# A two-layer decoder trunk on one core: gate and up with seven-product blocks over 14 of 16 k-tiles, w_down laid between them, one weight sum in four made by an adding transfer

## The chip, the core and the metric

The kernel runs on one core of one Trainium2 chip. The metric is the device time in microseconds (us), the median of several executions. In the profile the engines are PE (TensorE, the matrix products), PEld (its weight loads, which overlap it), DVE (VectorE), ACT (ScalarE), POOL (GpSimd) and SP (SyncE, which here only starts transfers). SBUF is the memory on the chip that the engines read; PSUM holds the eight banks into which PE adds up its products; DRAM holds the inputs.

## What is computed

The reference is a decoder of two layers over 256 tokens of width 2048, in fp32. Each layer has a mixer (layer 0: a Mamba-2 and a latent-attention group side by side; layer 1: stick-breaking attention) and a feed-forward part. Only the feed-forward part is changed in what PE does:

```
def swiglu_ffn(h, w_gate, w_up, w_down):
    return (jax.nn.silu(h @ w_gate) * (h @ w_up)) @ w_down

for layer in range(DEPTH):                    # DEPTH = 2
    h = rms_norm(x, mix_norm[layer])
    mix = ssd_mla_mixer(...) if layer % 2 == 0 else stick_breaking_mixer(...)
    x = x + mix
    x = x + swiglu_ffn(rms_norm(x, ffn_norm[layer]), w_gate[layer], w_up[layer], w_down[layer])
return rms_norm(x, final_norm)
```

`w_gate` and `w_up` are 2048 x 5632 in each layer, `w_down` is 5632 x 2048.

## The kernel before

**Tiles and products.** The 256 tokens are two row tiles of 128 (t = 0, 1). A width of 2048 is 16 k-tiles of 128. The hidden width of 5632 is 11 column groups of 512, n = 0 to 10. A weight piece is four k-tiles of 512 columns: 1 MB, a tile of 128 x 2048. All data is fp32, and PE multiplies words that are rounded to a shorter form (fp32r), so each piece is split: ACT casts it to its high part `wh` (L317), and DVE subtracts that from the piece, which leaves the low part in the piece's own buffer (L323). One product of a k-tile and 512 columns is three matmuls: high by `wh`, low by `wh`, high by the low part. What the text calls a product is one such matmul.

**Gate and up (`pair`).** For each column group the kernel makes four results of 128 x 512: gate and up, each for both row tiles. It looks on this as a 2 x 2 block product (two row tiles by two halves of the k-tiles, two halves by gate and up) and uses the seven products of Strassen's scheme in Winograd's form, M1 to M7, in place of eight. For this it needs four sums of weight pieces (L676, on DVE), which are split like pieces, and sums of the operands, made while the norm before is made. With b11, b21 for the two k halves of gate and b12, b22 for those of up, M1 takes b11, M3 b22 and M2 b21; M5 takes t1 = b12 - b11, M6 t2 = b22 - t1, M4 b21 - t2, and M7 b22 - b12, which is written over b12. The four accumulating banks are called z, p3, p2 and p4, a product's result goes to the bank of the results that need it, and what two results share is copied away from the bank in between by ACT (L750).

**How many k-tiles.** With the order HALF (n = 0, 1, 2) M1 to M7 cover 8 of the 16 k-tiles, and four pieces c0 to c3 with plain products the other eight. With MORE (n = 3 to 10) a second set of seven over 4 more k-tiles (n0 to n4, its half-piece sums t1 to t4) is added, and only c2 and c3 stay plain. With LATE `pair` serves the first columns of the two output projections. Seven blocks over 8 k-tiles are 7 x 4 k-tile products for the four results, where plain products would be 8 x 4.

**w_down.** The hidden activations h (L866 to L872: sum, silu, norm factor, product with up) are copied by a POOL transfer into a buffer of fp32r words (L875), transposed by PE (L328), split and kept as operands. `down` multiplies a pair of column groups (8 k-tiles) by one of the four column blocks of w_down: two pieces, 48 products (L423, L425, L426), then two copies out of PSUM on ACT (L890) and two adding transfers of 256 KB from SBUF into the DRAM buffers `saved` (L891). After each pair n from 2 to 9 two held projections follow. Behind the last pair, four projections of 12 k-tiles (72 products each) end the layer; the residual, which `residual_away` put into `saved`, comes back for them (`residual_back`).

**What sets the order.** PE runs the products in the order in which the code makes them. DVE, ACT, POOL and SP are ordered by a scheduler that follows priorities (`wprio` counts up with each weight piece, copies and h are urgent) and by the buffers: 4 for `wh`, 6 (7 in the feed-forward part) for pieces, 2 (3 in the feed-forward part, with a "lent" one) for sums. A piece's buffer comes free with the last product of its low part, and the next load or sum that gets that buffer waits for it.

## Time and profile before

| | |
|---|---|
| median of 3 runs | 2386.84 us (2384.85 to 2387.33) |
| profiled execution, span from first to last instruction | 2382.8 us |
| granted clock of PE, mean | 0.999 |
| PE busy | 2359.7 us, 99% |
| DVE busy | 1995.9 us, 84% |
| ACT busy | 1460.3 us, 61% |
| POOL busy | 234.9 us, 10% |
| moved by transfers | 497.87 MB, 209 GB/s over the span |

How to read it: a share of busy time is one over the whole span, with the mixers in it. A row of the groups of instructions names line, engine, operation, output<-input with shapes, count, then busy time and mean duration in ns, then the engine's idle time just before them and what ended it. A row of a timeline gives start, duration, engine and line, with the wait in front in brackets.

### The profile page before, as it was taken

How to read it: one execution, taken by the hardware profiler on the slowest of the kernel's cores; microseconds unless marked ns; L12 is line 12 of the kernel's file. 1: busy time of each engine (PE TensorE's matmuls, PEld its weight loads, DVE VectorE, ACT ScalarE, POOL GpSimd, SP SyncE). 2: the span in 40 equal slices, each digit the busy share in tenths (PEclk: the TensorE clock that was granted, in tenths of full speed). 3: DMA queues.
4: the chain of work that ended last, by engine and by line, in shares of the span. 5: the costliest groups of instructions: out<-in, count | busy, mean ns of one | idle time of the engine just before them, and what ended most of it. 6: DMA issues, size and time to landing. Idle time of an engine off the chain costs nothing.

```text
span 2382.8 us, 28019 instructions
## 1 busy us (share of the span) xinstructions
PE 2359.7 (99%) x10948; PEld 1956.2 (82%) x10948; DVE 1995.9 (84%) x1654; ACT 1460.3 (61%) x1476; POOL 234.9 (10%) x301
## 2 busy tenths in 40 slices
PE   8999999999999999999999999999999999999998
PEld 7888888887888888888888888888888888888886
DVE  6776587588997989989887889779998888999884
ACT  6665565565765655666665686775665565656663
POOL 1342011110000000000010010000000000000011
PEclk9999999999999999999999999999999999999999
DMA  7655556445667777777776555556667777777773
GB/s 265 198 187 195 181 194 191 127 142 177 230 212 231 222 225 232 231 226 231 225 251 204 203 177 176 177 177 230 230 225 209 237 230 225 226 228 234 226 257 114
DMA packets 274901, 497.87 MB, mean 209 GB/s; under 512 B 22924, under 2 KB 48144, under 8 KB 274768
## 3 DMA queue, kind: packets, MB, share of 16 engines
q1 hardware_dynamic: 255440, 446.48, 57.2%
q0 software_dynamic: 18752, 48.55, 7.7%
q8 instruction: 86, 1.41, 0.2%
q10 hardware_dynamic: 576, 1.05, 0.1%
q14 instruction: 47, 0.39, 0.0%
HBM read 459.24 MB, written 25.20 MB: 203 GB/s over the span
## 4 chain that ended last, share of the span: by engine, by line
PE 90%; issue 5%; ACT 1%; DMA 1%; DVE 1%; POOL 0%; SPq 0%; POOLq 0%; DVEq 0%; ACTq 0%
PE acc L729 51%; PE acc L423 11%; PE acc L426 11%; PE acc L425 11%; ACT wh L317 1%; PE at L1367 1%; PE tr L328 1%; PE tr L364 1%; PE at L1442 0%; DMA w<-in_w_in_dram 0%; PE at L1443 0%; PE tr L330 0%; DVE w L323 0%; POOL spare L1067 0%; DMA w<-in_w_out_even_dram 0%
## 5 line engine op out<-in xcount | busy, mean ns | idle before, releaser
L323 DVE TENSOR_TENSOR w<-w,wh 128x2048 fp32r<-128x2048 f32 (+2 forms) x399 | 893.7, 2247 | 185.3 <-ACT wh L317 176.3
L729 PE MATMUL acc<-wh,s 128*128 128x512 f32 x3896 | 986.3, 391 | 7.5 <-DVE s L323 3.1
L317 ACT CAST wh<-w 128x2048 fp32r<-128x2048 f32 (+2 forms) x399 | 744.6, 1874 | 347.3 <-PE acc L426 141.4
L729 PEld LDWEIGHTS acc<-wh,s 128*128 128x128 f32 x3896 | 725.4, 188 | 158.3 <-ACT s L750 4.9
L423 PE MATMUL acc<-wh,s 128*128 128x512 f32 (+1 forms) x1280 | 510.4, 399 | 1.3 <-ACT wh L317 1.3
L426 PE MATMUL acc<-wh,s 128*128 128x512 f32 (+1 forms) x1280 | 496.8, 388 | 0.0
L425 PE MATMUL acc<-w,s 128*128 128x512 f32 (+1 forms) x1216 | 471.0, 387 | 0.3 <-DVE w L323 0.3
L729 PE MATMUL acc<-w,s 128*128 128x512 f32 x1312 | 355.7, 389 | 0.2 <-DVE w L323 0.2
L729 PEld LDWEIGHTS acc<-w,s 128*128 128x128 f32 x1312 | 246.2, 188 | 52.1 <-DVE w L323 0.6
L426 PEld LDWEIGHTS acc<-wh,s 128*128 128x128 f32 x1280 | 240.6, 188 | 50.3
L423 PEld LDWEIGHTS acc<-wh,s 128*128 128x128 f32 x1280 | 240.9, 188 | 48.5 <-issue 1.7
L425 PEld LDWEIGHTS acc<-w,s 128*128 128x128 f32 x1216 | 229.1, 188 | 44.8 <-issue 1.7
L323 DVE TENSOR_TENSOR wsum<-wsum,wh 128x2048 fp32r<-128x2048 f32 (+1 forms) x101 | 218.4, 2162 | 6.3 <-ACT wh L317 6.3
L317 ACT CAST wh<-wsum 128x2048 fp32r<-128x2048 f32 (+1 forms) x101 | 182.8, 1810 | 45.6 <-PE acc L729 25.3
L317 ACT CAST wh<-lent 128x2048 fp32r<-128x2048 f32 (+1 forms) x62 | 114.5, 1857 | 63.2 <-DMA lent<-in_w_gate_dram 27.4
L323 DVE TENSOR_TENSOR lent<-lent,wh 128x2048 fp32r<-128x2048 f32 (+1 forms) x62 | 137.1, 2217 | 12.5 <-ACT wh L317 12.3
L676 DVE TENSOR_TENSOR wsum<-w,wsum 128x2048 f32<-128x2048 f32 (+1 forms) x52 | 104.0, 2001 | 23.3 <-PE acc L729 19.0
L750 ACT COPY s<-acc 128x512 f32<-128x512 f32 x132 | 77.4, 587 | 68.1 <-PE acc L729 68.1
L729 PE MATMUL acc<-wsum,s 128*128 128x512 f32 x380 | 104.6, 390 | 0.2 <-DVE wsum L323 0.2
L875 POOL DMA_DIRECT2D s<-s x44 | 24.5, 557 | 800.1 <-DVE s L872 418.0
L891 POOL DMA_DIRECT2D saved<-s x64 | 56.5, 1018 | 319.5 <-ACT s L890 319.5
L729 PEld LDWEIGHTS acc<-wsum,s 128*128 128x128 f32 x380 | 71.2, 188 | 15.9 <-DVE wsum L323 1.0
(264 smaller groups left out, 1852.4 us busy)
## 6 DMA issues: line engine op xcount, KB each, us to landing
w<-in_w_down_dram SPq DMA_DIRECT2D x80, 1024.0 KB, 5.0
w<-in_w_gate_dram SPq DMA_DIRECT2D x76, 1024.0 KB, 5.2
w<-in_w_up_dram SPq DMA_DIRECT2D x76, 1024.0 KB, 5.2
w<-in_w_qkv_dram SPq DMA_DIRECT2D x48, 1024.0 KB, 5.0
w<-in_w_in_dram SPq DMA_DIRECT2D x47, 1024.0 KB, 5.1
w<-in_w_out_even_dram SPq DMA_DIRECT2D x32, 1024.0 KB, 5.0
saved<-s POOLq DMA_DIRECT2D x64, 256.0 KB, 7.3
w<-in_w_out_odd_dram SPq DMA_DIRECT2D x16, 1024.0 KB, 5.0
```

Source lines behind the costliest of these rows:

```text
L317: cast = nc.scalar.copy(hi, src).ins
L323: return nc.vector.tensor_tensor(lo, src, hi.bitcast(F32), op=ALU.subtract).ins
L328: self.nc.tensor.transpose(out.bitcast(F32R), src, self.ident_r)
L364: self.nc.tensor.transpose(pt[:, k, t * P:(t + 1) * P], src(t, 2 * k2 + k), self.ident)
L423: nc.tensor.matmul(ps[t], hi[:, ts], wh, start=k == 0, stop=False)
L425: slot.used(nc.tensor.matmul(ps[t], hi[:, ts], wl, start=False, stop=False), self.clock)
L426: nc.tensor.matmul(ps[t], lo[:, ts], wh, start=False, stop=k == nk - 1)
L676: ins = self.nc.vector.tensor_tensor(half(o, so), half(p, sp), half(q, sq), op=ALU.subtract).ins
L729: m = nc.tensor.matmul(ps[b], x, y, start=b not in started, stop=stop, skip_group_check=True)
L750: self.kept = nc.scalar.copy(o, ps[b]).ins
L875: nc.gpsimd.dma_start(words.bitcast(F32), h[t])
L891: nc.gpsimd.dma_start(self.saved[n][:, t], s, accum_op=ALU.add)
```

## The change

**Gate and up.** The pairs n = 0 and 1 keep HALF. From n = 2 on, the order MOST takes 14 k-tiles by sevens: M1 to M7 over 8 k-tiles as before, and N1 to N7 over 6 more with pieces of three k-tiles (128 x 1536). The last two k-tiles of gate and of up are one plain piece (c2). All sums of a pair that DVE makes (L709 now) are full (M) or three-quarter (N) pieces; each holds a sum buffer or a piece's buffer.

**The adding transfer.** M7 now takes b12 + b22: once DVE has made t1 = b12 - b11, `wadd` (L703) starts a transfer on POOL that adds b22 from DRAM straight into b12's buffer. The sum on DVE that made M7's weights goes. t2 becomes b22 + t1, and signs in the operand sums follow from it.

**w_down in between.** "d" in the order stands for half a projection of w_down (one piece, 24 products, L907 to L910), with PSUM banks of the kind "tr", which the transposes used too; "h" and "H" are the places where the transposes of the h before are asked for (even and odd n). The projections over the groups 8 and 9 for the column blocks 2 and 3 are made in pair 10, so behind it two projections stay at 72 products and two shrink to 24.

**h.** `Twin` gives the same bytes two names, one of fp32 and one of fp32r; DVE writes h there (L880), and PE transposes it from there (L354) without the POOL copy. Two small buffers of the rope moved into new space.

**The order of the instructions.** DVE before, in a step with MORE: `wsum10`, `wsum11` and `lent0` are the buffers of sums, `w5`, `w7` of pieces, `wh` of high parts. The row with L676 is the sum for M4.

```order
L323 TENSOR_TENSOR wsum10_81<-wsum10_82,wh3_68 128x2048
L323 TENSOR_TENSOR w5_71<-w5_72,wh0_65 128x2048
L676 TENSOR_TENSOR wsum10_82<-w7_76,wsum11_84 128x2048
L323 TENSOR_TENSOR wsum11_83<-wsum11_84,wh1_66 128x2048
L323 TENSOR_TENSOR w7_75<-w7_76,wh2_67 128x2048
L323 TENSOR_TENSOR wsum10_81<-wsum10_82,wh3_68 128x2048
```

The sum is written over M5's low part; behind it stand the splits of M6, M2 and M4. DVE after, at the second half of the pair n = 6; `w6` (first row) and `w5` hold the second and third w_down piece:

```order
L348 TENSOR_TENSOR w6_73<-w6_74,wh1_66 128x2048
L709 TENSOR_TENSOR lent0_90<-w4_70,wsum10_82 128x2048
L348 TENSOR_TENSOR wsum10_81<-wsum10_82,wh2_67 128x2048
L348 TENSOR_TENSOR w4_69<-w4_70,wh0_65 128x2048
L348 TENSOR_TENSOR w5_71<-w5_72,wh1_66 128x2048
L709 TENSOR_TENSOR wsum10_82<-w9_80,wsum11_84 128x1536
L348 TENSOR_TENSOR wsum11_83<-wsum11_84,wh3_68 128x1536
L348 TENSOR_TENSOR w7_75<-w7_76,wh2_67 128x2048
```

The first L709 row is the sum for M4, the second that for N4. The latter is written over the low part of M6 (`wsum10`, split in the third row), and stands behind the split of the third w_down piece and ahead of the split of N6 (`wsum11`, 128 x 1536). PE at the same place (`s` are the operands, `acc` the banks; the rows begin with M6's low part):

```order
L763 MATMUL acc_6989<-wsum_81,s_599_4772 128x512 x4
L763 MATMUL acc_6989<-wh_68,s_651_5313 128x512
L763 MATMUL acc_6989<-wh_68,s_652_5314 128x512
L763 MATMUL acc_6989<-wh_68,s_654_5330 128x512
L763 MATMUL acc_6989<-wh_68,s_655_5331 128x512
L763 MATMUL acc_6989<-wh_68,s_657_5345 128x512
L763 MATMUL acc_6989<-wh_68,s_658_5346 128x512
L763 MATMUL acc_6989<-wsum_83,s_651_5313 128x512
L763 MATMUL acc_6989<-wsum_83,s_654_5330 128x512
L763 MATMUL acc_6989<-wsum_83,s_657_5345 128x512
L763 MATMUL acc_6991<-wh_65,s_593_4738 128x512
```

Six high products of N6 now stand between M6's last low product and N6's first low one. DVE after, a little earlier in the same pair, around the first w_down piece (`w9`, split in the third row):

```order
L709 TENSOR_TENSOR wsum11_84<-lent1_92,lent0_90 128x1536
L348 TENSOR_TENSOR s2_754_7033<-tr_752_7027,s2_753_7032 128x512
L348 TENSOR_TENSOR w9_79<-w9_80,wh1_66 128x2048
L348 TENSOR_TENSOR s2_757_7042<-tr_755_7036,s2_756_7041 128x512
L348 TENSOR_TENSOR lent0_91<-lent0_90,wh2_67 128x1536
L348 TENSOR_TENSOR w5_71<-w5_72,wh3_68 128x2048
L348 TENSOR_TENSOR lent1_93<-lent1_92,wh0_65 128x1536
```

The first row is the sum for N6, written over M5's low part (`wsum11`); the two 512-column rows split the transposed h. On PE the order around it is M5, h, N1, d, N5, M3, N3.

The diff, cut to its core:

```
+class Twin:
+    def __init__(self, raw, words):
+        self.raw, self.words, self.writer, self.last = raw, words, None, None
...

+    def wadd(self, o, view, k0, n=4):
+        with self.priority(self.wprio):
+            self.wprio += 100
+            for dst, w in view(o.raw, k0, k0 + n):
+                self.nc.gpsimd.dma_start(dst, w, accum_op=ALU.add)

-    MORE = ("M1", "M5", "c2", "t1", "t2", "t4", "n0", "n2", "n4", "M3", "M6", "M2", "t3", "M4", "n1", "M7", "n3", "c3")
+    MOST = ("M1", "M5", "h", "N1", "d", "N5", "M3", "N3", "d", "M6", "N6", "M2", "d", "M7", "N7", "M4", "N2", "N4",
+            "H", "c2", "d")
...
+        first, size = {"M": 0, "N": 8}, {"M": 4, "N": 3}
...
+            if m in ("h", "H", "d"):
+                if m in then:
+                    then[m]()
+                continue
...
+            if m == "1":
+                b11, b12, b22 = (raw[q + c] for c in ("b11", "b12", "b22"))
+                t1, t2 = self.wsum(), self.wsum()
...
+                self.wsub(t1, b12, b11, n)
+                self.wadd(b12, vb, first[q] + n, n)
+                if more and q == "M":
+                    load("N", "b11", "b12", "b22")
+            if m == "5":
+                self.wsub(src[q + "6"], src[q + "3"], src[q + "5"], n, ALU.add)
+            if m == "6":
+                load(q, "b21")
+                src[q + "2"], src[q + "4"] = raw[q + "b21"], self.wsum()
+                self.wsub(src[q + "4"], src[q + "2"], src[q + "6"], n)
+            keep = m in "1567" and (q == "N" or not more)
+            add(bank[m], ops(q, m), self.wsplit(src[q + m], n, n), keep and m)
...
-            if m == "M3":
-                self.wsub(b12, b22, b12, after=st["lo"] if after == "lo" else after)
...
-            words = self.s2([512], F32R)
-            nc.gpsimd.dma_start(words.bitcast(F32), h[t])
-            h[t] = words
+            twin = self.twins[t]
+            self.wrote(twin, nc.vector.scalar_tensor_tensor(twin.raw, s, rstd[:, t:t + 1], h[t],
+                                                            op0=ALU.mult, op1=ALU.mult).ins)
...
+            if n > 1 and n % 2 == 0:
+                steps += [down(acts[n - 2:n], n - 2, c) for c in range(0 if n < last else 2, 4)]
...
+                      self.MOST if n > 1 else self.HALF, then)
...
+            r0 = 8 if n < 2 else 10
-            if n == 2:
+            if n == 3:
                 st["more"] = self.spawn(self.more_sums(st))
```

`steps` holds the halves of the projections that are left to make (`step` takes the next one at each "d"); `self.after` and `self.wrote` name the dependences of the two names of h, which the scheduler can't see.

## The prediction

> **What bounds the kernel now.** I read the page first (share of each engine, clock), then the chain of waits, then the stretch of one gate/up step by windows and by timeline.

> ```profile
> span 2382.8 us, 28019 instructions
> ...
> PE 2359.7 (99%) x10948; PEld 1956.2 (82%) x10948; DVE 1995.9 (84%) x1654; ACT 1460.3 (61%) x1476; POOL 234.9 (10%) x301
> ...
> PEclk9999999999999999999999999999999999999999
> ```

> PE is busy nearly the whole span at full clock in every slice; 2382.8 - 2359.7 leaves 23.1 us in which it is idle. The windows answer for one later gate/up step (columns after each window: busy time of PE, PEld, DVE, ACT and POOL with counts, clock, DMA share, GB/s), and the chain's piece for its products:

> ```profile
> 828.87:890.83 61.96, 61.96 (x279) 51.31 (x279) 56.21 (x34) 37.56 (x29) 4.66 (x6) 1.00 0.74 229
> ```

> ```profile
> 828.87 39.44 PE acc L729 x174
> ```

> 174 products take 39.44 us: 0.2267 us each. The step is 174 gate/up products and 96 of w_down (61.2 us) and eight transposes, so PE never waits in it. DVE, at 56.21 of 61.96 us, has 6 us to spare: it is the second bound, and what it does late PE feels at once. The waits of PE over the whole span:

> ```profile
> PE acc L729 <- DVE s L323: 3.1, 2, 2.4
> PE acc L729 <- ACT s L750: 2.7, 4, 1.2
> ```

> These are the costliest of the products' waits. The kernel is PE-bound; a product saved is worth 0.2267 us, and a wait put in front of a product costs its full length.

> **What is saved.** A pair in seven-product blocks over 14 k-tiles has 7x4 + 7x3 + 2x4 = 57 k-tile products of three matmuls, 171; over 12 k-tiles it has 7x4 + 7x2 + 4x4 = 58, 174; over 8 it has 60, 180. Before: three pairs at 180 and eight at 174, 1932 a layer; after: two at 180 and nine at 171, 1899. 33 matmuls a layer, 66 in all, x 0.2267 = **15.0 us saved**. The transposes and w_down products keep their number.

> **What DVE gains or loses.** Durations by shape, and the pitch in a full stretch:

> ```profile
> L323 DVE TENSOR_TENSOR w<-w,wh 128x2048 fp32r<-128x2048 f32 x383 | 876.7, 2296 | 179.0 <-ACT wh L317 170.1 <-DMA w<-in_w_ukv_dram 5.6 <-DMA w<-in_w_uq_dram 1.4
> L676 DVE TENSOR_TENSOR wsum<-w,wsum 128x1024 f32<-128x1024 f32 x14 | 17.1, 1225 | 5.8 <-PE acc L729 5.5
> ```

> ```profile
> 843.86 2.29 DVE L676 TENSOR_TENSOR wsum<-w,lent 128x2048 f32<-128x2048 f32 x1 [1.49 <-PE acc L729]
> 846.07 2.28 DVE L323 TENSOR_TENSOR lent<-lent,wh 128x2048 fp32r<-128x2048 f32 x1
> 848.27 2.29 DVE L323 TENSOR_TENSOR w<-w,wh 128x2048 fp32r<-128x2048 f32 x1
> ```

> A 2048-column instruction holds DVE for 2.20 us (start to start), a 1024 one about 1.13; 1536 columns, which no row shows, lie between: 1.67 us held, 1.76 to its end (both halfway). Before, a step with two w_down projections has 16 full and one half split and 4 full and 4 half sums: 49.6 us. After: 12 full and 7 three-quarter splits, 3 full and 3 three-quarter sums: 33.0 + 16.7 = 49.7 us. Moving one sum in four to a transfer pays for the larger second block and no more, so DVE's 6 us of spare time stay as they were; what counts is the order.

> **Where PE will wait, step one (N6).** Before, the sum for M4 waits for a slot of the sums and DVE then splits M6. In the rows above it starts at 843.86, and M6's split ends at 848.35. PE meanwhile:

> ```profile
> 843.21 0.61 PE L729 MATMUL acc<-wsum,s 128*128 128x512 f32 x2
> 843.66 1.07 PE L729 MATMUL acc<-wh,s 128*128 128x512 f32 x4
> 844.57 0.61 PE L729 MATMUL acc<-w,s 128*128 128x512 f32 x2
> 845.02 1.98 PE L729 MATMUL acc<-wh,s 128*128 128x512 f32 x8
> 846.84 1.07 PE L729 MATMUL acc<-lent,s 128*128 128x512 f32 x4
> 847.74 1.98 PE L729 MATMUL acc<-wh,s 128*128 128x512 f32 x8
> 849.56 0.62 PE L729 MATMUL acc<-lent,s 128*128 128x512 f32 x2
> ```

> The slot is free at about 843.7, and PE needs the split's low part only at 849.56, after 26 other products: 1.2 us in hand. After the change the sum for N4 waits for M6's last product, since with three sum slots M6's is the only one free, and the very next product is N6, whose split stands behind that sum on DVE. Its cover is six high products, 1.36 us, instead of 26. In front of that sum stands the split of the third w_down piece, which waits for its cast on ACT; that cast reuses the buffer of the second piece and stands behind the two copies of w_down's result:

> ```profile
> 1002.50 1.27 ACT L890 COPY s<-acc 128x512 f32<-128x512 f32 x2 [2.80 <-PE acc L426]
> 1003.66 1.92 ACT L317 CAST wh<-wsum 128x2048 fp32r<-128x2048 f32 x1
> ```

> From the last product of the second w_down piece, t = 0: the second copy until 0.65 (the first lies under the last products), the cast until 2.56, the split holds DVE until 4.76, N4's sum until 6.43, N6's split ends at 8.2. PE runs M6 (12) and N6's high products (6) until 18 x 0.2267 = 4.1. **Wait 4.1 us.** Without the w_down split in front, the sum would start when M6 ends, 2.7, and the wait be 2.7 + 1.67 + 1.76 - 4.1 = 2.1: the low end; 4.6, with half a microsecond of lateness on ACT, is the high one. I take 4.1, as the order leaves no other path.

> **Step two (first w_down piece).** N6's own sum is written over M5's slot: it waits for M5's last product (t = 0), holds DVE until 1.7, and the split of the first w_down piece behind it ends at 4.0. PE has N1 (9) and one w_down product, 10 x 0.2267 = 2.3, and then needs the low part: 1.7 us. Where h is transposed at that place (even pairs), its eight transposes give PE 0.8 more (61.96 - 61.2) and a 512-column split, about 0.6, comes first on DVE; I take 1.8 for all, 1.0 to 3.8, the high end if the piece itself lands 2 us late.

> **Step three (bank p3).** N5's result is copied away and the next product, M3, writes the same bank. In the PE waits above, four such waits took 2.7 us, 0.68 each, the copy itself 0.59. I take 0.65 (0.4 to 1.2). Before, half-products of other banks stood between.

> Together 4.1 + 1.8 + 0.65 = 6.55 us for each of 18 pairs, **118 us**. Since PE has no slack to win back, it all goes into the span.

> **The adding transfer.** Nothing in the trace adds 1 MB from DRAM into SBUF. The nearest rows:

> ```profile
> w<-in_w_down_dram SPq DMA_DIRECT2D x80, 1024.0 KB, 5.0
> ...
> saved<-s POOLq DMA_DIRECT2D x64, 256.0 KB, 7.3
> ```

> and what the two queues move in the step of the window above (packets, MB, share of sixteen engines):

> ```profile
> q1 hardware_dynamic: 6336, 12.58, 62.1%
> q0 software_dynamic: 736, 1.57, 11.6%
> ```

> Low end 5.0 us (a plain load), high end four times the adding 256 KB, 29 us. I take 11.5: 7.3 and another 768 KB at 187 GB/s. That rate: POOL's queue (q0) has 11.6% of 61.96 us, 7.2 us; its 0.52 MB of plain copies at the load queue's 327 GB/s (12.58 MB in 38.5 us) take 1.6, and 1.05 MB of adding is left with 5.6. M7 follows M1 by 168 products, 38 us, in the new order; by 96, 22 us, in the pairs with eight k-tiles; by 60, 13.6 us, in the three pairs at the start of an output projection. So 0 is taken; 29 us would cost up to 18 us in each of those three. On POOL each such transfer waits for the first sum, and what is queued behind it (the two `saved` transfers, the last head group's rope) waits too: no product follows from `saved` before the layer's end; the rope can lose a load and a sum, 5.0 + 2.3, at most, and I take 0.

> **The rest.** The h copies go; PE waited for none of them and POOL is 10% busy, so 0. The signs of the sums and the new places of the rope's buffers change no instruction, 0. The third piece of the operand sums falls in the first two pairs, where DVE is fullest:

> ```profile
> 640.00:700.00 60.00, 60.00 (x271) 49.68 (x270) 59.48 (x46) 39.17 (x32) 1.09 (x2) 1.00 0.65 213
> ```

> It adds some 2.5 us there and the adding transfer takes 2.2 us out of each pair: 0 to 5 a layer, 2 taken. At the layer's end two of the four projections shrink from 72 to 24 products, so the next layer's sums have 10.9 us of cover instead of 32.6, for about 8 us of DVE work: 1 taken, 0 to 3. Together 6 us.

> Sum: 2382.8 - 15.0 + 118 + 6 = 2491.8 us of span. The median, 2386.84, stands 4.0 above the span shown: **2496 us**. A measurement of this kernel tells 0.2%, about 5 us, from no change.

> **The rivals.**
> (a) Shorter chain. The third piece's cast is early, so N6 waits 2.1, the first piece 1.0, the bank 0.4: 3.5 x 18 = 63, and 2386.8 - 15 + 63 + 6 = 2441. For it: most waits of DVE on ACT are short. Against: the cast cannot start before the buffer is free.
> (b) Late transfers. The queues take 73.7% of a step. 1.8 MB more by adding is about 9.7 us of all sixteen engines, the copies of h give 1.6 back, and it becomes some 87% of the old step, and the loads of w_down pieces, issued one step ahead of their use, come some 3 us late: 18 x 3 = 54, 2550. [...]

> ```profile
> lent<-in_w_gate_dram SPq DMA_DIRECT2D x1, 1024.0 KB, 5.8
> ```

> (c) The clock. The granted clock was 1.00 through waits of up to 2.4 us; a wait of 4.1 is not in the trace. If it halved the clock for as long as the wait, 4.1 us of products would take 2.05 more: 18 x 2.05 = 37, 2533. [...] The trace neither shows nor excludes it.
> (d) Faster. If DVE runs far enough ahead that N4's sum is never late, only the saved products are left: 2386.8 - 15 = 2372. It decides at 15.0 / 18 = 0.83 us of wait a pair. For it: no wait in today's steps; against: the sum can't run ahead of M6's last product, whatever DVE's lead. If the waits come out near 0.83, the time stays within 0.2%.

> **How the numbers follow.** Forecast 0.60 (its own range 2455 to 2535), (a) 0.12, (b) 0.13, (c) 0.08, (d) 0.04, no change 0.03. Faster 0.04, same 0.03, slower 0.93. The range reaches below (a) and above (b): 2425 to 2570.

> **What would show it.** Right: in the windows a step of 67 to 69 us instead of 62 with some 6.5 us of PE idle in it; among PE's waits the split line (now L348) on wsum about 18 times at 4 us, the same line on a w_down piece 18 times near 2, the copy line 18 times near 0.65; DVE 55 us a step. Wrong: steps of 61.3 us with PE idle under 1 us; PE or ACT waiting for an adding transfer (rival b); granted clock under 1.00 (rival c).

## The result, and the profile after

The changed kernel took 2603.51 us (median of 4 runs, 2598.34 to 2607.62) against 2386.14 us before: 1.0911 times as long, 95% interval 1.0896 to 1.0927. Slower was forecast, and the waits that it named are in the trace, but 2496 us and at most 2570 were given, and the sum held no price for the clock. The loss is 217 us where 109 were expected.

The page of the changed kernel, span, busy time of each engine, clock and the two main transfer queues:

```profile
span 2605.9 us, 28253 instructions
...
PE 2428.0 (93%) x10882; PEld 1986.1 (76%) x10882; DVE 1989.8 (76%) x1671; ACT 1495.3 (57%) x1524; POOL 281.4 (11%) x316
...
PEclk9999999999999999999999999999999999999999
...
q1 hardware_dynamic: 256016, 446.48, 51.7%
q0 software_dynamic: 41008, 87.87, 17.2%
```

Two things are to be seen. PE's idle time grew from 23.1 to 2605.9 - 2428.0 = 177.9 us, 154.8 more. And PE's busy time grew too, by 68.3 us, though it has 66 instructions less and 15 us of products were saved. The row of the clock shows nothing of it: a tenth rounds the loss away. The view of the cores does:

```profile
core 0: 2605.9 us, clock 0.969
```

Before, that number was 0.999. PE's waits over the whole span:

```profile
PE acc L763 <- DVE wsum L348: 73.3, 18, 4.1
PE tr L909 <- DVE w L348: 38.9, 18, 2.9
PE acc L763 <- ACT s L784: 28.5, 24, 6.8
...
PE tr L907 <- ACT wh L342: 3.0, 6, 1.5
```

The first row is step one (N6), 18 times 4.07 us. The second and fourth are step two (first w_down piece), 41.9 us or 2.3 a pair. The third holds step three, 18 copies at about 0.68 us, two waits of 6.8 us at the start of the third pair, and the four that before had. ACT at one of the two long waits, with the cast of an operand sum ahead of the copy that PE needs:

```profile
703.00 0.62 ACT L342 CAST s<-s 128x512 fp32r<-128x512 f32 x1 [5.09 <-DVE s L538]
703.52 0.58 ACT L784 COPY s<-acc 128x512 f32<-128x512 f32 x1
```

DVE makes that sum at 702.68, at the end of a stretch of 15 us without a gap. One pair of waits in the timeline, DVE first, then PE (in brackets: the wait ahead of the row, and what ended it):

```profile
1108.63 2.29 DVE L348 TENSOR_TENSOR w<-w,wh 128x2048 fp32r<-128x2048 f32 x1 [4.31 <-ACT wh L342]
1110.84 1.75 DVE L709 TENSOR_TENSOR lent<-w,wsum 128x1536 f32<-128x1536 f32 x1
1112.51 1.75 DVE L348 TENSOR_TENSOR wsum<-wsum,wh 128x1536 fp32r<-128x1536 f32 x1
```

```profile
1107.82 1.07 PE L763 MATMUL acc<-lent,s 128*128 128x512 f32 x4
1108.73 1.52 PE L763 MATMUL acc<-wh,s 128*128 128x512 f32 x6
1114.32 1.65 PE L763 MATMUL acc<-wsum,s 128*128 128x512 f32 x3 [4.07 <-DVE wsum L348]
1115.76 3.61 PE L763 MATMUL acc<-wh,s 128*128 128x512 f32 x8
1119.18 1.35 PE L763 MATMUL acc<-w,s 128*128 128x512 f32 x4
```

This is the predicted chain, instruction by instruction: the split of the third w_down piece, held up by its cast on ACT, then N4's sum, then N6's split; PE stands after six high products. Next to look at is what follows the wait: eight high products take 3.42 us from start to start, 0.427 each, where they took 1.81 elsewhere in the same step. The windows over that stretch, and over the one behind the wait for the first w_down piece of that pair, give the granted clock (the number behind POOL):

```profile
1114.32:1119.20 4.88, 4.88 (x12) 3.82 (x13) 3.35 (x2) 1.96 (x2) 0.00 (x0) 0.50 0.01 3
1086.00:1088.72 2.72, 2.72 (x6) 2.15 (x7) 2.72 (x2) 2.65 (x2) 0.00 (x0) 0.50 1.09 263
```

PE runs at half clock behind the wait. In the first window DVE is busy for 3.35 of 4.88 us and the queues carry 3 GB/s, in the second they carry 263; the clock is 0.50 in both. All 18 waits before N6 are followed by such products, 5 to 13 each.

Over the span 282 products start 0.38 to 0.44 us apart instead of 0.227; before there were 14. That is 268 x 0.2 = 54 us. The steps show both losses together, a step of 62 us having become one of about 72:

```profile
970.00:1041.75 71.75, 64.29 (x283) 52.20 (x283) 56.74 (x36) 39.97 (x33) 6.11 (x6) 0.98 0.77 216
1041.75:1114.32 72.57, 64.48 (x268) 51.94 (x268) 54.33 (x32) 38.14 (x29) 6.13 (x6) 0.95 0.76 214
```

DVE's work stayed at 54 to 57 us a step, near the 55 of the forecast. The adding transfers landed like this:

```profile
w<-in_w_up_dram POOLq DMA_DIRECT2D x22, 1024.0 KB, 10.8
```

11.5 us had been taken from two nearest rows. No wait of PE is put down to one of them.

### The profile page after: what moved, and what is told of

Same layout as the page of the kernel before. It is cut to its first block, busy times and chain, and to the rows that moved or that the text cites. A ratio compares the mean times of both kernels' runs of the same rounds, so it can differ in the third digit from the quotient of the medians.

```text
span 2605.9 us, 28253 instructions
## 1 busy us (share of the span) xinstructions
PE 2428.0 (93%) x10882; PEld 1986.1 (76%) x10882; DVE 1989.8 (76%) x1671; ACT 1495.3 (57%) x1524; POOL 281.4 (11%) x316
## 3 DMA queue, kind: packets, MB, share of 16 engines
q10 hardware_dynamic: 576, 1.05, 0.1%
## 4 chain that ended last, share of the span: by engine, by line
PE 78%; DVE 9%; issue 5%; DMA 4%; ACT 4%; POOL 0%; ACTq 0%; SPq 0%; DVEq 0%; POOLq 0%
PE acc L763 39%; PE acc L450 6%; PE acc L453 6%; PE acc L452 6%; PE tr L909 5%; PE tr L910 5%; PE tr L907 5%; DVE w L348 3%; ACT wh L342 3%; DMA w<-in_w_down_dram 2%; DVE wsum L348 2%; DVE wsum L709 1%; DMA w<-in_w_qkv_dram 1%; DVE lent L709 1%; DMA w<-in_w_out_odd_dram 1%
## 5 line engine op out<-in xcount | busy, mean ns | idle before, releaser
L348 DVE TENSOR_TENSOR w<-w,wh 128x2048 fp32r<-128x2048 f32 (+3 forms) x411 | 891.2, 2177 | 352.1 <-ACT wh L342 343.2
L342 ACT CAST wh<-w 128x2048 fp32r<-128x2048 f32 (+3 forms) x411 | 740.3, 1818 | 401.2 <-PE tr L910 127.9
L763 PEld LDWEIGHTS acc<-wh,s 128*128 128x128 f32 x3852 | 735.3, 193 | 206.2 <-ACT s L784 38.6
L450 PE MATMUL acc<-wh,s 128*128 128x512 f32 (+1 forms) x704 | 284.2, 404 | 1.1 <-ACT wh L342 1.1
L453 PE MATMUL acc<-wh,s 128*128 128x512 f32 (+1 forms) x704 | 272.6, 387 | 0.0
L452 PE MATMUL acc<-w,s 128*128 128x512 f32 (+1 forms) x704 | 272.1, 387 | 0.0
L909 PE MATMUL tr<-w,s 128*128 128x512 f32 x576 | 234.1, 406 | 38.9 <-DVE w L348 38.9
L348 DVE TENSOR_TENSOR wsum<-wsum,wh 128x2048 fp32r<-128x2048 f32 (+1 forms) x115 | 243.8, 2120 | 27.2 <-ACT wh L342 27.2
L763 PEld LDWEIGHTS acc<-w,s 128*128 128x128 f32 x1154 | 220.2, 191 | 48.1 <-DVE w L348 0.6
L907 PE MATMUL tr<-wh,s 128*128 128x512 f32 x576 | 231.9, 403 | 3.2 <-ACT wh L342 3.0
L910 PE MATMUL tr<-wh,s 128*128 128x512 f32 x576 | 231.5, 402 | 0.0
L763 PE MATMUL acc<-wsum,s 128*128 128x512 f32 x424 | 128.9, 426 | 73.3 <-DVE wsum L348 73.3
L348 DVE TENSOR_TENSOR lent<-lent,wh 128x1536 fp32r<-128x1536 f32 (+1 forms) x76 | 154.6, 2034 | 24.6 <-ACT wh L342 24.6
L909 PEld LDWEIGHTS tr<-w,s 128*128 128x128 f32 x576 | 112.5, 195 | 69.3 <-DVE w L348 45.5
L453 PEld LDWEIGHTS acc<-wh,s 128*128 128x128 f32 x704 | 132.8, 189 | 27.7
L450 PEld LDWEIGHTS acc<-wh,s 128*128 128x128 f32 x704 | 133.0, 189 | 27.0 <-issue 1.7
L452 PEld LDWEIGHTS acc<-w,s 128*128 128x128 f32 x704 | 133.2, 189 | 25.2 <-issue 1.4
## 6 DMA issues: line engine op xcount, KB each, us to landing
w<-in_w_down_dram SPq DMA_DIRECT2D x88, 1024.0 KB, 5.8
w<-in_w_gate_dram SPq DMA_DIRECT2D x52, 1024.0 KB, 5.4
w<-in_w_up_dram SPq DMA_DIRECT2D x50, 1024.0 KB, 5.1
w<-in_w_qkv_dram SPq DMA_DIRECT2D x48, 1024.0 KB, 5.1
w<-in_w_in_dram SPq DMA_DIRECT2D x47, 1024.0 KB, 5.1
w<-in_w_out_even_dram SPq DMA_DIRECT2D x32, 1024.0 KB, 5.1
w<-in_w_up_dram POOLq DMA_DIRECT2D x22, 1024.0 KB, 10.8
```

The source lines that it names most:

```text
L342: cast = nc.scalar.copy(hi, src).ins
L348: return nc.vector.tensor_tensor(lo, src, hi.bitcast(F32), op=ALU.subtract).ins
L450: nc.tensor.matmul(ps[t], hi[:, ts], wh, start=k == 0, stop=False)
L452: slot.used(nc.tensor.matmul(ps[t], hi[:, ts], wl, start=False, stop=False), self.clock)
L453: nc.tensor.matmul(ps[t], lo[:, ts], wh, start=False, stop=k == nk - 1)
L763: m = nc.tensor.matmul(ps[b], x, y, start=b not in started, stop=stop, skip_group_check=True)
```

## The experiments

**Theory:** the loss is the waits that the new order makes, at the three places and at the start of the third pair, and slow products behind the longer ones, because PE stood still. **Rivals:** the adding transfers crowd the queues and make pieces late; N6 is late for another reason than the sum's buffer; the products are slow for another reason than the wait.

**1. N6 behind M2.** Two neighbours of the order change places:

```
-    "M6", "N6", "M2", "d", "M7",
+    "M6", "M2", "N6", "d", "M7",
```

> In the order of a pair N6 and M2 change places. Theory (N4's sum waits for the last low product of M6, behind the split of the third w_down piece, and each wait that is long enough is followed by products at half the clock): the 12 products of M2 now cover 2.7 us of the 4.2 us wait in front of N6's low products, so 1.4 to 1.5 us of it stay in each of 18 pairs, 49 us less; and a wait so short is not followed by slow products, of which 145 stand behind the 18 waits of the changed kernel, 0.2 us each: 29 us less. Together 2525, range 2510 to 2545. Rival, short chain (the w_down split is not what delays the sum): the wait goes wholly, about 2498. Rival, late transfers (the waits come from the load of the queues): the order between the same transfers matters little, 2590 or more.

Measured: 2527.96 us (2527.54 to 2531.3), 1.0594 of before (1.0578 to 1.061). PE's wait, and the place in the timeline:

```profile
PE acc L763 <- DVE wsum L348: 24.3, 18, 1.3
```

```profile
1091.33 1.52 PE L763 MATMUL acc<-wh,s 128*128 128x512 f32 x6
1094.20 0.96 PE L763 MATMUL acc<-wsum,s 128*128 128x512 f32 x3 [1.34 <-DVE wsum L348]
```

M2's 12 products, 2.72 us, came off the wait and left 4.07 - 2.72 = 1.35: so the w_down split does stand in the chain, and the short chain falls. Behind 1.34 us of wait no product is slow (three in 0.96, not 1.65). 49 us of waits and 25 of slow products (155 are left of 282) make up nearly all of the 75.5 us.

**2. The wait filled.** 18 products that nothing reads, ahead of N6's low ones:

```
+            if fill:
+                idle = self.tr([512])
+                for k in range(fill):
+                    nc.tensor.matmul(idle, x[0][0], wh[:, 0], start=k == 0, stop=k == fill - 1)
```

> Ahead of N6's low products PE gets 18 products (4.1 us) whose result nothing reads, so that it works through the wait. Theory (the half clock comes from PE standing still): the wait before N6 is filled, which gains nothing by itself, and the 145 slow products behind it run at full clock: 29 us less, 2575, range 2562 to 2588; the first w_down piece keeps its wait and its slow products. Rival (the products behind the wait are slow for another reason, such as late weight loads or a crowded SBUF): no change or slower, 2600 to 2610.

Measured: 2571.97 us (2568.3 to 2574.01), 1.0774 (1.0758 to 1.079). The wait for N6 is gone from the list, the first piece's is as it was, and the clock of a whole step, in which N6's place lies, is full:

```profile
PE tr L913 <- DVE w L348: 38.5, 18, 2.9
...
1041.00:1112.00 71.00, 68.30 (x298) 55.34 (x298) 54.86 (x32) 39.59 (x30) 6.14 (x6) 1.00 0.78 223
```

324 useless products made the kernel 31.5 us faster. They replace time in which PE stood, and with it the slow products behind N6's place went; the load of the queues, which stayed (223 GB/s in this window, 214 in that step of the changed kernel, at a clock of 0.95), did not make them.

**3. The sum back on DVE.** No adding transfer in the whole kernel:

```
-                self.wadd(b12, vb, first[q] + n, n)
+            if m == "3":
+                self.wsub(src[q + "7"], src[q + "7"], src[q + "3"], n, ALU.add)
```

> The adding transfers are left out; DVE makes b12 + b22 itself, ahead of M3's split, in every pair of the whole kernel. Theory (the waits are those of the order, and the adding transfers are hidden): the waits at the three places stay at 4.2, 2.0 to 3.1 and 0.8 us, and the time stays within 15 us of 2603, DVE having some 14 us a step to spare now. Rival (the 39 MB that the adding transfers move beside the loads delay w_down's pieces): the first w_down piece's wait falls below 1 us and the time by 30 to 60 us, to 2545 to 2575.

Measured: 2582.81 us (2578.0 to 2592.54), 1.0834 (1.0808 to 1.086).

```profile
PE acc L763 <- DVE wsum L348: 73.2, 18, 4.1
PE tr L910 <- DVE w L348: 39.0, 18, 3.0
PE acc L763 <- ACT s L784: 22.8, 23, 4.1
```

The waits at N6 and at the first piece did not move at all, so the adding transfers are not their cause, and late transfers fall as the main cause. The time moved by 20.7 us, 6 more than allowed for. 5.7 of it is the third row, the shorter wait at the third pair's start. 14 us are slow products: 212 instead of 282, most of the difference behind the first w_down piece, where the same waits were followed by slow products in 3 pairs of 18 here and in 10 of 18 with the adding transfers. In run 1, with the same waits there and the adding transfers, it was 15 of 18. In the trace of the changed kernel the slow products go with the place of a wait on a grid of 3.413 us (last section), and a kernel with other times has its waits at other places; so these 14 us are not put down to the adding transfers. The executions of this one kernel differ with the clock too: 2578.0 us at a mean clock of 0.978, 2592.54 at 0.973.

**4. A fourth buffer for sums.**

```
-        for slot, tag in zip(self.lent, ("wsum", "w")):
+        for slot, tag in zip(self.lent, ("wsum", "wsum")):
```

> Both lent buffers of the feed-forward part serve sums, so that there are four for sums and six for pieces (three and seven before). Theory: N4's sum no longer has to wait for M6, and the 4.2 us wait in front of N6 goes in all 18 pairs with its slow products, 76 + 29 us; with a buffer less for pieces the loads start later and the first w_down piece may wait 1 to 3 us longer, 18 to 54 us with some slow products, so 2500 to 2570. Rival (it is the split of the third w_down piece or DVE's load that delays N6, not the sum buffer): N6's wait stays above 2 us in PE's list of waits.

Measured: 2612.3 us (2610.73 to 2618.06), 1.0949 (1.0931 to 1.0967), a miss of 42 us. PE's waits, and ACT at the first w_down piece of a pair:

```profile
PE tr L907 <- ACT wh L342: 107.2, 18, 8.3
PE tr L909 <- DVE w L348: 27.6, 18, 1.5
```

```profile
1097.12 1.90 ACT L342 CAST wh<-w 128x2048 fp32r<-128x2048 f32 x1 [5.69 <-DMA w<-in_w_down_dram]
```

N6's wait is gone from the list, as the theory has it: the sum no longer waits for M6, so the buffer was the cause. But a buffer less for pieces made w_down's first piece late by 107.2 us in all, twice what I had allowed, and the run has 231 slow products, at a mean clock of 0.961. Here the trade of one kind of buffer for the other lost 9 us more than it gained.

**5. Another order.** The same products, sums and transfers:

```
+    MOST = ("M1", "M5", "N1", "N5", "h", "H", "d", "M3", "N3", "M6", "d", "M2", "d", "N6", "M4",
+            "M7", "N7", "N2", "N4", "c2", "d")
```

> Only the order of a pair is another: M1 M5 N1 N5 h H d M3 N3 M6 d M2 d N6 M4 M7 N7 N2 N4 c2 d, the same products, sums and transfers. Theory (the loss is all in the three places and in the slow products behind them): N6 has M2 and a w_down half in front of it, the copies of N5 and N6 have work of other banks behind them, and the first w_down piece has 19 products and eight transposes for cover, so N6's and the banks' waits go and 0.4 to 1.5 us a pair stay at the first piece. Before's 2388, less 15 us of products, plus 18 x 0.7 = 13, plus the wait at the start of the third pair that is left as it is (two times 7 us and some 20 slow products, 18), plus 6 for the rest: 2410, range 2395 to 2430. Rival, late transfers: the waits go to other places and the time stays above 2470.

Measured: 2425.98 us (2425.26 to 2427.26), 1.0162 (1.0148 to 1.0176).

```profile
PE acc L763 <- ACT s L784: 16.4, 6, 6.9
PE tr L909 <- DVE w L348: 8.4, 18, 1.8
```

178 of the 217 us are gone with nothing but an order. What is left in the first row are the two waits at the third pair's start (6.9 and like it) and the four that before had too.

**6. That, and the operand sums asked for later.**

```
-        yield 40
+        yield 56
...
-        if more and "more" in st:
-            self.join(st["more"])
...
+            if q == "N" and m == "5" and "more" in st:
+                self.join(st["more"])
```

> As the run with the new order, and the three operand sums of the second block are begun 16 ticks later and asked for at N5 instead of at the pair's start. Theory (the 7 us at the start of the third pair come from those sums standing ahead of the copy of a bank on ACT and ahead of the splits on DVE): that wait falls below 1.5 us, 12 to 18 us less than the run with the new order: 2394, range 2382 to 2404. Rival (DVE is simply full in the first two pairs, and the work only comes due later): the wait shows up inside the third pair, and the two runs differ by less than 5 us.

Measured: 2407.88 us (2406.64 to 2410.86), 1.0087 (1.0073 to 1.0101): 18 us less than with the order alone, as the theory has it, though 4 us over the range.

```profile
PE tr L909 <- DVE w L348: 5.5, 18, 0.4
...
PE acc L761 <- ACT s L782: 2.7, 4, 1.2
...
PE acc L761 <- DVE lent L348: 2.0, 2, 1.0
```

```profile
968.00:1030.20 62.20, 61.78 (x276) 50.68 (x275) 55.14 (x34) 38.71 (x32) 6.11 (x6) 1.00 0.87 248
1030.20:1092.50 62.30, 61.88 (x276) 50.72 (x276) 54.98 (x34) 38.74 (x33) 6.12 (x6) 1.00 0.88 251
```

The wait at the start is gone, the copies' row is before's own, and what is left of it is 1.0 us at N5's low part, where the sums are now asked for. (Beginning them later and asking for them later were not tried apart.) A step is 62.2 us at full clock, against 61.96 before: the three products saved, 0.68 us, are spent on what is left of the waits. So the change loses 21 us even here: PE is idle for 45.3 us, where it was 23.1 before, and its busy time is 2362.0 us, no less than before's 2359.7.

**7. The order, and the operand sums on POOL** (`nc.gpsimd` for `nc.vector` in the twelve small subtractions of `more_sums`).

> As the run with the new order, and the twelve small operand subtractions of the second block are made by POOL instead of DVE. Theory: DVE gets 3 us a layer back where it is full, the wait at the start of the third pair falls below 2 us, 12 to 18 us less than the run with the new order: 2394, range 2382 to 2406. Rival: POOL, which takes longer for each and stands behind its transfers, makes the sums late, and the pair waits as long as now or longer, 2405 to 2425.

Measured: 2421.72 us (2419.01 to 2424.39), 1.0144 (1.013 to 1.0158): 4 us less than with the order alone, so the rival's range.

```profile
PE acc L763 <- ACT s L784: 12.2, 6, 4.8
```

Taking the work off DVE shortened the wait from 6.9 to 4.8 us; asking for it later ended it (run 6). In this run the cast ahead of the copy waits for POOL's sums instead (3.53 us at 699.45), so it does not tell how much of the wait was DVE's load. Run 6 shows that the place of the sums ahead of an urgent copy was enough to make it.

**8. Run 6 without adding transfers** (the edit of run 3).

> As the run with the new order and the late join, but without the adding transfers: DVE makes b12 + b22 ahead of M3's and N3's splits. Where the pair was full of waits this moved the time by 20 us, down. Theory (DVE is the second bound, and without waits it has no room): the two sums, 2.2 and 1.7 us, stand in front of splits that PE needs soon and are felt in part, 0 to 3.9 us a pair, about half taken: 35 us more than the run with the adding transfers, range 10 to 70 more. Rival (the adding transfer buys nothing, as 6 us of DVE are free): within 8 us of that run.

Measured: 2442.51 us (2439.72 to 2447.84), 1.0234 (1.022 to 1.0248), 34.6 more than run 6; 35 had been expected.

```profile
PE tr L910 <- DVE w L348: 19.3, 36, 0.8
PE acc L761 <- DVE wsum L348: 14.4, 18, 1.3
...
968.00:1032.00 64.00, 61.55 (x273) 49.80 (x272) 59.89 (x37) 39.39 (x32) 3.49 (x4) 1.00 0.68 210
```

DVE is at 59.89 of 64 us. So the adding transfer earns its place, 35 us, in an order without waits. In the changed kernel the version without it was 21 us faster, and DVE had some 15 us a step to spare.

## Why the prediction was wrong, point by point

- **Products saved, 15.0 us.** 66 instructions less on PE, and the two k-tile counts as worked out. Right.
- **Step one, N6, 4.1 us.** 4.07 in the trace, by the same chain, and by runs 1 and 4 for the stated reasons. Right: 73.3 us for 73.8.
- **Step two, 1.8 us.** 2.3. In the range, under-sized by 10 us in all. The forecast's chain has no term for the piece's cast (only its high end allowed for a late piece), and in 17 of the 18 pairs ACT waits with that cast for the piece to land:

```profile
ACT wh L342 <- DMA w<-in_w_down_dram: 94.0, 17, 10.2
```

  Between N6's sum and the end of the piece's split DVE stands idle for 0.2 to 1.7 us in 17 pairs, 13 us in all, waiting for ACT. Without adding transfers (run 3) this row has 103.9 us and 18 waits, so they are not what makes the piece late.
- **Step three, 0.65 us.** 0.68. Right.
- **The adding transfer, 0.** No wait of PE is put down to it; run 3 leaves the waits at N6 and at the first piece as they are. Right for the feed-forward part's steps. (The `lent` load with 5.8 us under rival (b) is one load of w_gate; the same load one step later, with as many `saved` transfers beside it, took 5.2, the median of before's 12 such loads.)
- **The rest, 6 us.** Here a term of the sum was mis-sized. Under "the third piece of the operand sums" 0 to 5 us a layer were given and 2 taken, by adding up DVE's spare time. Measured were 6.8 us at the start of the third pair of each layer, and slow products behind it; run 6 takes 18 us away. The sums are asked for at the pair's start and so stand ahead of an urgent copy of a bank: a place in a queue was priced by the load of an engine. Some 14 us more of idle time lie in small waits elsewhere.
- **The clock.** This is the step that failed: the forecast took a wait of PE to cost its full length and no more. The price of the clock stood among the rivals, as (c) with a chance of 0.08 (the author's estimate; no row of before shows it), as though either the clock changed or the forecast held. But (c)'s condition was met by the forecast's own step one: whoever takes 4.1 us of wait for certain has to put the price of such a wait into the sum. With it the forecast would have been (c)'s 2533. The size was short too: the slow products cost 54 us and not 37, as they came not only behind N6 (145 of them, 29 us) but behind the first w_down piece and at the third pair's start, which (c) didn't count.
- **What the sum comes to.** 2382.8 - 15.0 + 154.8 (idle) + 54 (slow products) = 2576.6, and the span is 2605.9. Of the other 29 us about 16 are the last product ahead of each of some 100 more waits, which the profile counts as busy for 0.39 us where its successor would have followed after 0.23. About 13 are products only partly at half clock: in the trace's clock records PE is busy for 133.5 us of the stretches at half clock, which costs half of that, 66.8 us, where the count by products has 54. Against the forecast's span of 2491.8 the clock is thus the largest of what is missing, ahead of 31 us of idle time (154.8 for 118 + 6).

## What to carry to other kernels

Where PE is busy for 99% of the span, a rearrangement that saves products can't be priced until each shared buffer's release has been followed to the instruction that needs it next: here new waits, the largest of them for a buffer freed by the product just before, made a saving of 15 us a loss of 217, and another order of the same work gave 178 back. A wait of PE can cost more than its length: here the 4.07 us before N6 cost another 1.6 us each in slow products, run 1's 1.34 us nothing more, so the sum of a forecast needs a term for them. What takes load off an engine (the adding transfer) shows its worth only after the waits are gone, so it can't be judged by taking it out of a kernel that waits.

## What the runs showed of the hardware that was not expected

Behind some waits of PE the granted clock was 0.50, for 5 to 13 products of 0.427 us behind N6's: after 1.34 us in run 1 never (18 waits); at the first w_down piece, 1.1 to 3.3 us, in 3 (run 3), 10 (the changed kernel) or 15 (run 1) pairs of 18; after 4.07 us in all 18. With useless products in the wait (run 2) the clock of the step was 1.00. The wait of 4.07 us before N6 thus cost 29 / 18 = 1.6 us more than its length.

```profile
1109.51:1112.93 3.42, 0.74 (x4) 0.28 (x2) 3.42 (x3) 0.90 (x1) 0.00 (x0) 1.00 1.08 242
1112.93:1116.34 3.41, 2.02 (x5) 1.64 (x6) 3.41 (x2) 0.34 (x1) 0.00 (x0) 0.50 0.28 52
1116.34:1119.75 3.41, 3.41 (x10) 2.64 (x9) 1.88 (x2) 1.90 (x3) 0.00 (x0) 0.50 0.00 0
1119.75:1123.17 3.42, 3.42 (x17) 2.81 (x16) 1.76 (x1) 1.62 (x1) 0.00 (x0) 1.00 0.42 99
```

PE is idle for 2.7 us of the first window, and the next one has a clock of 0.50; in that one it is idle for 1.4 us, and the one behind it has 0.50 too; behind a window without idle time the clock is 1.00 again. Two waits at the first w_down piece, of 2.87 and of 2.74 us:

```profile
867.17:870.58 3.41, 1.59 (x7) 0.94 (x6) 2.28 (x3) 3.41 (x5) 0.00 (x0) 1.00 1.08 256
870.58:873.99 3.41, 2.36 (x10) 1.98 (x11) 3.41 (x4) 3.41 (x3) 0.00 (x0) 1.00 1.10 263
873.99:877.41 3.42, 3.42 (x16) 2.82 (x16) 3.42 (x2) 0.38 (x2) 0.00 (x0) 1.00 1.00 362
...
2048.18:2051.59 3.41, 0.79 (x3) 0.67 (x4) 3.41 (x4) 3.41 (x4) 0.00 (x0) 1.00 1.10 262
2051.59:2055.01 3.42, 3.42 (x9) 2.63 (x8) 3.42 (x2) 1.75 (x2) 0.00 (x0) 0.50 1.07 304
```

The longer wait is cut in two by the grid, 1.82 and 1.05 us, and the clock stays at 1.00; of the shorter one 2.62 us lie in one window, and the next has 0.50. Over this trace, from its first clock record on (13.8 us after the start) and with the ends of products as the profile models them, 34 windows at full clock were followed by half clock, the least idle of them with 1.820 us; of the 678 that were followed by full clock the most idle had 1.817. From half clock, 33 windows were followed by full clock, with at most 0.51 us idle, and 13 by half clock, with at least 0.60. No run moved one wait along the grid with all else kept, so that its place is the cause is inferred from these counts.

A transfer that adds 1 MB from DRAM to SBUF landed 10.8 us after its issue in the changed kernel (median of 22), where the plain loads of 1 MB from w_up took 5.1 and those from w_down 5.8; 40 adding transfers in the feed-forward part (22 of 1 MB, 18 of 768 KB, which took 13.0) lay beside the loads, and no wait of PE is put down to one.
